# A third seven-product pair in the mixer and attention blocks, with sums of weights made by adding transfers

## The chip, the cores and the metric

The kernel runs on one core of a Trainium2 chip. The metric is the device time of one execution in microseconds (us), the median over several runs. The engines are named as the profile names them: PE (TensorE, with PEld for the loading of its stationary operand), DVE (VectorE), ACT (ScalarE), POOL (GpSimd) and SP (SyncE). SP, ACT and POOL also issue transfers.

## The reference

A decoder trunk of two layers over 256 positions of width 2048, all in float32:

```python
for layer in range(2):
    xn = rms_norm(x, norm_mix[layer])
    x = x + (mixer_mlstm_ssd if layer == 0 else mixer_moba)(xn, ...)
    h = rms_norm(x, norm_ffn[layer])
    x = x + (silu(h @ gate) * (h @ up)) @ down        # 2048 -> 5632 -> 2048
return rms_norm(x, final_norm)
```

Layer 0's mixer projects the normed input with one matrix of 2048 x 12336 (mLSTM queries, keys, values and output gate, two gate rows, and the x, z, B, C and dt columns of a Mamba-2 scan), computes both kinds of heads over chunks, norms and gates them, and multiplies the 4096 resulting columns by one output matrix. Layer 1's mixer is attention with 16 heads and rotary positions; as its blocks are 256 long and there are 256 positions, it is plain causal attention. The work is mostly matrix products of 256 rows with large weight matrices that are read once from memory.

## The kernel before, in words

**Blocks.** Each large product is cut into blocks: the 256 tokens against two strips of 512 columns of a weight matrix (or one strip of each of two matrices), over a depth of 2048 (three feed-forward chunks of 2048, 2048 and 1536 for the down product). `block` (L296) does one. Its depth is cut into pairs of two 128-row tiles; a plan, a string in `PLAN` (L37), has a letter for each pair.

**Precision.** A float32 operand is split into a high part (rounded to the type that TensorE takes, a cast on ACT, L269) and the rest (a subtraction on DVE, L274). A product takes three matmuls of 128 x 128 by 512 columns: high x high, high x low, low x high (`add`, L303 to L307).

**P pairs.** A pair with the letter P has 2 tiles x 2 token halves x 2 strips, that is 8 products, summed in four PSUM banks (`acc_f`).

**S pairs.** A pair with the letter S takes its 2 x 2 x 2 products as one product of 2 x 2 matrices with a seven-product scheme: sums of weights and sums of activations go in, 3 of the products go to `acc_f`, 4 to banks of their own (`acc_e`, L330 to L333). After the last S of a block these four are combined into four tiles `pre` (L335 to L342), and after the block's last pair the `acc_f` banks are added to them (`gathered`, L382). The four `acc_e` banks are those that small products otherwise use in turn (`aux_bank`).

**Weights of a pair** (`weights`, L250). SP loads the pair's weights into two tiles `raw` (six buffers). An S pair needs two first sums of weight tiles, `sums` (two buffers). In the feed-forward parts, where the flag `in_transfers` is set (L942), these come from transfers: SP loads one tile into `sums` (L259), and POOL issues a second transfer that adds another tile onto it (L260); one tile of `raw` is then not loaded (L263). Elsewhere DVE adds them from `raw` (L283). Two more sums (L287, L289) are DVE's in both cases. Then come the casts and subtractions into `wh` and `wl` (six buffers each). These run with a raised priority.

**Sums of activations.** An S pair also needs four sums of the activations' token halves, split into high and low (`activation_sums`, L234), kept in a tile `sk`. They are made once for each pair of a matrix's depth, either when the activations are transposed (L218 to L226) or when an S first asks for them (`summed`, L200). The tiles come from shared homes: `sk` has 3 buffers, `s` 10, `vh` 2, and working tiles (`t2`) 9.

**Order.** Blocks run in this order: two B/C blocks (plan bc), four x/z blocks (xz), qk0, two halves of the first output product (w1), v0, o, qk1, v1, o, two halves of the second output product (w2); feed-forward; av0, aq, aq, av1, aq, aq, two halves of the attention's output product (wo); feed-forward. Smaller work (transposes, convolutions, decays, scores, softmax) is put off with `later` by a number of pairs; after each pair `tick` (L175) runs what is due. From the first S of a block to its last, nothing that was put off runs (`held`), as the banks are taken; it runs after the next pair. Within these orders a scheduler places instructions on each engine by priority, and each engine and queue works through its list in order.

**What lies around the change.** For the mLSTM, `decay_rows` (L653) allocates a tile, issues two transfers on POOL (L657) that spread two rows of cumulated gates over all partitions, and adds a mask on DVE (L661). `mlstm_scores` (L793) calls it and then applies the exponential and the scores. In attention, `rope_block` rotates queries and keys (L979 to L985), `qk_pair` transposes them two pairs later, `attend` makes scores and softmax three and four pairs later (L1010 to L1021), `attend_turn` transposes the probabilities and `attend_out` multiplies by the values, each a pair later; its output is the input `o` of the wo blocks. A norm's square root is taken on POOL (L141).

Of the kernel before, what the change touches and what calls it, by code (L numbers as in the profile page):

```python
# [38 lines left out]
    "v0": "PPPSPSPP", "o": "PPPSPSPP", "qk1": "PPPSPSPP", "v1": "PPPSPSPP", "w2": ("PPPSPSPP", "PPPSPSPP"),  # L39
    "x": "PSPSPSSP", "x0": "PPPSPSSP", "down4": ("PSPSPSSP", "PSPSPSSP"), "down3": ("PSPSPP", "PSPSPP"),  # L40
    "av0": "PPPSPSPP", "aq": "PPPSPSPP", "av1": "PPPSPSPP", "wo": ("PPPPPPPP", "PPPSPSPP"),
# [20 lines left out]
def hybrid_trunk(ctx: ExitStack, tc: tile.TileContext, a: dict, out: bass.AP):  # L62
    nc = tc.nc
# [94 lines left out]
    in_transfers = [False]  # L158
# [91 lines left out]
    def weights(src, row, summed):  # L250
# [6 lines left out]
        if summed and in_transfers[0]:  # L257
            for i, other in enumerate((unit(wa, row + P, ca), unit(wb, row, cb))):
                nc.sync.dma_start(sums[:, i, :], unit(wb, row + P, cb))  # L259
                nc.gpsimd.dma_start(sums[:, i, :], other, accum_op=OP.add)  # L260
        nc.sync.dma_start(raw[0], pair(wa, ca))
        if summed and in_transfers[0]:
            nc.sync.dma_start(raw[1][:, 0, :], unit(wb, row, cb))  # L263
        else:
            nc.sync.dma_start(raw[1], pair(wb, cb))
# [11 lines left out]
        with tc.high_priority(offset=800), tied(last[0], cast[0], *also):  # L277
            if not summed:
                return [low(*parts(r)) for r in raw]
            a, b = raw  # L280
            if not in_transfers[0]:
                for i, other in enumerate((a[:, 1, :], b[:, 0, :])):
                    nc.vector.tensor_add(sums[:, i, :], b[:, 1, :], other)  # L283
            pa = parts(a)
            ps = parts(sums)
            b21, b11 = low(*pa)
            nc.vector.tensor_add(b[:, 1, :], b[:, 0, :], sums[:, 0, :])  # L287
            pb = parts(b)
            nc.vector.tensor_add(a[:, 0, :], a[:, 0, :], b[:, 1, :])  # L289
            t1, t3 = low(*ps)  # L290
            pt = parts(a, 1)
            b22, t2_ = low(*pb)
            t4, = low(*pt)
            return b21, b11, b22, t3, t1, t2_, t4
# [481 lines left out]
    vh, em = {}, {}  # L776
# [4 lines left out]
    def v_block(g, plan, wait):  # L781
        for i in range(2):
            later(wait + i, ("e", g), mlstm_scores, g, i)
# [9 lines left out]
    def mlstm_scores(g, i):  # L793
        need(("qk", g))
        es = decay_rows(4 * g + 2 * i, s_home)
        em[2 * g + i] = es
# [101 lines left out]
    def ffn(xt, r, wg_, wu_, wd, name, finish, begin=None):  # L898
# [43 lines left out]
        in_transfers[0] = True  # L942
# [9 lines left out]
        in_transfers[0] = False  # L952

    xt2, ss2, finish_ffn0 = next_x("2", G_MIX1, {1: sk_home, 3: sk_home, 5: sk_home})
# [205 lines left out]
```

## Time and profile before

| | |
|---|---|
| runs | 2546.05, 2547.03, 2551.55 us; median 2547.03 |
| the profiled execution | 2547.64 us, of which the trace's span is 2545.9 |
| PE busy | 2534.9 us (100%) |
| DVE busy | 2236.4 us (88%) |
| ACT busy | 1571.5 us (62%) |
| POOL busy | 283.7 us (11%) |
| moved | 593.72 MB, 233 GB/s on average |

The span is that of the core's instructions; some 1.7 us of the time lie around it. A row by stretches gives start and end, its length, busy time of PE, PEld, DVE, ACT and POOL with the number of instructions behind each, the granted clock of PE, the share of time in which the 16 DMA engines were busy, and GB/s. A row of a group gives line, engine, operation, output and inputs, shape, count, then busy us and mean ns, then the idle time before it with what ended it. A row of waits gives who waited for whom: us in total, times, longest. A row of the timeline starts with its start and its length in us. Matmuls are pipelined: one shows about 390 ns, while the next starts before it ends, so that their pace is read from their starts or their count.

### The profile page before, as it was taken

Reading aid. Unit: us, or ns where it says so; the run is one execution under the profiler, and the core shown is the slowest. Engines: PE = TensorE matmul, PEld = TensorE weight load, DVE = VectorE, ACT = ScalarE, POOL = GpSimd, SP = SyncE. Lnnn points to the kernel's source line nnn. Section 1 sums busy time; section 2 is a strip of 40 time slices with the busy share of each in tenths; the row PEclk is TensorE's granted clock in tenths of the full one; section 3 lists DMA queues with packets and bytes.
Section 4 is the critical chain, followed back from the end, with each engine's and each line's share of the span. In section 5 each row is a group of like instructions: output and inputs, shape, how many; then the busy total and the mean of one; then the engine's idle time right before and its main releaser. Section 6 shows DMA issues by size and latency. Waiting matters only on the chain.

```text
span 2545.9 us, 34058 instructions
## 1 busy us (share of the span) xinstructions
PE 2534.9 (100%) x11595; PEld 2090.3 (82%) x11595; DVE 2236.4 (88%) x2995; ACT 1571.5 (62%) x2108; POOL 283.7 (11%) x356
## 2 busy tenths in 40 slices
PE   9999999999999999999999999999999999999998
PEld 8888888888888888888888888888888888888887
DVE  6877789887799999999999989878899999999998
ACT  6566766565666665666566655656566656665664
POOL 2101200000001111111111000000011111111110
PEclk9999999999999999999999999999999999999999
DMA  8656656566578999999999756555689999999995
GB/s 282 184 166 190 197 165 218 178 189 212 158 219 238 276 271 285 277 282 264 287 271 280 249 174 196 176 163 176 203 224 283 262 288 279 275 272 289 290 270 169
DMA packets 312158, 593.72 MB, mean 233 GB/s; under 512 B 24184, under 2 KB 26752, under 8 KB 311984
## 3 DMA queue, kind: packets, MB, share of 16 engines
q1 hardware_dynamic: 271248, 515.12, 61.3%
q0 software_dynamic: 39552, 74.58, 16.6%
q8 instruction: 91, 1.49, 0.2%
q10 hardware_dynamic: 1184, 1.84, 0.2%
q14 instruction: 83, 0.68, 0.1%
HBM read 589.32 MB, written 2.14 MB: 232 GB/s over the span
## 4 chain that ended last, share of the span: by engine, by line
PE 94%; issue 3%; DVE 2%; DMA 1%; ACT 0%; POOL 0%; POOLq 0%; DVEq 0%; ACTq 0%
PE acc_f L305 24%; PE acc_f L307 24%; PE acc_f L306 24%; PE acc_e L305 6%; PE acc_e L307 5%; PE acc_e L306 5%; PE p_tr L215 1%; PE p_y L727 1%; DVE wl L274 1%; PE p_qt L772 0%; PE p_num L815 0%; DMA raw<-in_l_ffn_down 0%; PE p_cv L468 0%; PE p_o L1036 0%; PE p_qk L1008 0%
## 5 line engine op out<-in xcount | busy, mean ns | idle before, releaser
L269 ACT CAST wh<-raw 128x1024 fp32r<-128x1024 f32 (+1 forms) x1070 | 1041.7, 989 | 676.6 <-PE acc_f L307 298.2
L274 DVE TENSOR_TENSOR wl<-raw,wh 128x1024 fp32r<-128x1024 f32 (+1 forms) x1070 | 1206.5, 1142 | 203.7 <-ACT wh L269 193.0
L305 PE MATMUL acc_f<-wh,x 128*128 128x512 f32 x1204 | 472.2, 392 | 0.0
L306 PE MATMUL acc_f<-wl,x 128*128 128x512 f32 x1204 | 471.2, 391 | 0.0
L307 PE MATMUL acc_f<-wh,x 128*128 128x512 f32 x1204 | 471.0, 391 | 0.0
L305 PE MATMUL acc_f<-wh,xa 128*128 128x512 f32 x708 | 281.2, 397 | 0.0
L307 PE MATMUL acc_f<-wh,xa 128*128 128x512 f32 x708 | 276.5, 391 | 0.0
L306 PE MATMUL acc_f<-wl,xa 128*128 128x512 f32 x708 | 276.4, 390 | 0.0
L307 PEld LDWEIGHTS acc_f<-wh,x 128*128 128x128 f32 x1204 | 226.2, 188 | 46.4
L306 PEld LDWEIGHTS acc_f<-wl,x 128*128 128x128 f32 x1204 | 226.2, 188 | 46.3
L305 PEld LDWEIGHTS acc_f<-wh,x 128*128 128x128 f32 x1204 | 226.3, 188 | 45.8
L269 ACT CAST wh<-sums 128x1024 fp32r<-128x1024 f32 x160 | 168.6, 1054 | 143.3 <-PE acc_f L307 71.3
L274 DVE TENSOR_TENSOR wl<-sums,wh 128x1024 fp32r<-128x1024 f32 x160 | 195.3, 1221 | 18.4 <-ACT wh L269 18.4
L260 POOL DMA_DIRECT2D sums<-in_l_ffn_gate x86 | 74.6, 868 | 1135.0 <-DVE wl L274 491.4
L305 PE MATMUL acc_e<-wh,sk 128*128 128x512 f32 x480 | 190.2, 396 | 0.0
L306 PE MATMUL acc_e<-wl,sk 128*128 128x512 f32 x480 | 187.4, 390 | 0.0
L307 PE MATMUL acc_e<-wh,sk 128*128 128x512 f32 x480 | 186.5, 391 | 0.0
L307 PEld LDWEIGHTS acc_f<-wh,xa 128*128 128x128 f32 x708 | 132.9, 188 | 28.1
L306 PEld LDWEIGHTS acc_f<-wl,xa 128*128 128x128 f32 x708 | 133.2, 188 | 26.9 <-DVE wl L274 0.4
L305 PEld LDWEIGHTS acc_f<-wh,xa 128*128 128x128 f32 x708 | 133.1, 188 | 26.0
L287 DVE TENSOR_TENSOR raw<-raw,sums 128x512 f32<-128x512 f32 x160 | 109.6, 685 | 7.9 <-DMA sums<-in_l_ffn_down 4.9
L305 PEld LDWEIGHTS acc_e<-wh,sk 128*128 128x128 f32 x480 | 90.1, 188 | 28.4 <-ACT xg L221 6.8
(337 smaller groups left out, 3981.6 us busy)
## 6 DMA issues: line engine op xcount, KB each, us to landing
raw<-in_l_w_in SPq DMA_DIRECT2D x192, 512.0 KB, 4.4
raw<-in_l_ffn_gate SPq DMA_DIRECT2D x176, 512.0 KB, 6.3
raw<-in_l_ffn_down SPq DMA_DIRECT2D x136, 512.0 KB, 6.8
raw<-in_l_w_qkv SPq DMA_DIRECT2D x96, 512.0 KB, 4.6
raw<-in_l_ffn_up SPq DMA_DIRECT2D x90, 512.0 KB, 6.3
sums<-in_l_ffn_up SPq DMA_DIRECT2D x172, 256.0 KB, 4.6
raw<-in_l_w_out SPq DMA_DIRECT2D x64, 512.0 KB, 4.8
sums<-in_l_ffn_gate POOLq DMA_DIRECT2D x86, 256.0 KB, 6.6
```

The source lines that it names most:

```text
L215: turned = nc.tensor.transpose(pt[:, i * T + t * P:i * T + (t + 1) * P], src[t][:, i * P:(i + 1) * P], ident)
L260: nc.gpsimd.dma_start(sums[:, i, :], other, accum_op=OP.add)
L269: cast[0] = nc.scalar.copy(h[:, :n, :], of[:, :n, :]).ins
L274: last[0] = nc.vector.tensor_sub(l[:, :n, :], of[:, :n, :], h[:, :n, :].bitcast(F32)).ins
L287: nc.vector.tensor_add(b[:, 1, :], b[:, 0, :], sums[:, 0, :])
L305: nc.tensor.matmul(dst, ah, bh, start=start, stop=False, **kw)
L306: nc.tensor.matmul(dst, ah, bl, start=False, stop=False, **kw)
L307: nth[0] = nc.tensor.matmul(dst, al, bh, start=False, stop=stop, **kw).ins
L727: nc.tensor.matmul(py[:, o0:o0 + SHD], e[:, lo:lo + P], y[:, st, hs], start=st == 0, stop=st == t, skip_group_check=True)
```

## The change: what it does

Three things, in one edit. First, the flag `in_transfers` goes: every S pair, in mixer and attention too, gets its two first sums of weights by adding transfers, and the DVE additions of L283 go. Second, the plans: fourteen blocks change from two S (pairs 3 and 5) to three (pairs 3, 5 and 6): v0, both o, qk1, v1, both w2, av0, the four aq, av1 and the second wo. The first wo block changes from no S to two, in pairs 1 and 2. As the attention input's pairs 3, 5 and 6 are now the S pairs there, `next_x("2", ...)` makes sums of activations for these and no longer for pair 1. Third, `v_block` calls `decay_rows` for both head pairs ahead of its block, and `mlstm_scores` takes the tile from there.

```diff
 PLAN = {
     "bc": "PPPPPPPP", "xz": "PPPPPPPP", "qk0": "PPPPPPPP", "w1": ("PSPSPSPP", "PSPSPSPP"),
-    "v0": "PPPSPSPP", "o": "PPPSPSPP", "qk1": "PPPSPSPP", "v1": "PPPSPSPP", "w2": ("PPPSPSPP", "PPPSPSPP"),
+    "v0": "PPPSPSSP", "o": "PPPSPSSP", "qk1": "PPPSPSSP", "v1": "PPPSPSSP", "w2": ("PPPSPSSP", "PPPSPSSP"),
     "x": "PSPSPSSP", "x0": "PPPSPSSP", "down4": ("PSPSPSSP", "PSPSPSSP"), "down3": ("PSPSPP", "PSPSPP"),
-    "av0": "PPPSPSPP", "aq": "PPPSPSPP", "av1": "PPPSPSPP", "wo": ("PPPPPPPP", "PPPSPSPP"),
+    "av0": "PPPSPSSP", "aq": "PPPSPSSP", "av1": "PPPSPSSP", "wo": ("PSSPPPPP", "PPPSPSSP"),
 }
...
         if summed:
             sums = home("sum")([P, 2, STRIP], "sums")
-        if summed and in_transfers[0]:
             for i, other in enumerate((unit(wa, row + P, ca), unit(wb, row, cb))):
                 nc.sync.dma_start(sums[:, i, :], unit(wb, row + P, cb))
                 nc.gpsimd.dma_start(sums[:, i, :], other, accum_op=OP.add)
         nc.sync.dma_start(raw[0], pair(wa, ca))
-        if summed and in_transfers[0]:
+        if summed:
             nc.sync.dma_start(raw[1][:, 0, :], unit(wb, row, cb))
...
             a, b = raw
-            if not in_transfers[0]:
-                for i, other in enumerate((a[:, 1, :], b[:, 0, :])):
-                    nc.vector.tensor_add(sums[:, i, :], b[:, 1, :], other)
             pa = parts(a)
...
     def v_block(g, plan, wait):
         for i in range(2):
+            em[2 * g + i] = decay_rows(4 * g + 2 * i, s_home)
             later(wait + i, ("e", g), mlstm_scores, g, i)
...
     def mlstm_scores(g, i):
         need(("qk", g))
-        es = decay_rows(4 * g + 2 * i, s_home)
-        em[2 * g + i] = es
+        es = em[2 * g + i]
...
-    xt2, ss2, finish_ffn0 = next_x("2", G_MIX1, {1: sk_home, 3: sk_home, 5: sk_home})
+    xt2, ss2, finish_ffn0 = next_x("2", G_MIX1, {3: sk_home, 5: sk_home, 6: sk_home})
```

More of the change, by code (lines that the diff above doesn't have):

```diff
@@ L157, in hybrid_trunk @@
     also, evacuated = [], []
-    in_transfers = [False]
     last, cast, nth, fresh = [None], [None], [None], [None, None]
@@ L940, in down @@
                         finish(s)
-        in_transfers[0] = True
         first = 0
@@ L951, in ffn @@
             first += n
-        in_transfers[0] = False
-    xt2, ss2, finish_ffn0 = next_x("2", G_MIX1, {1: sk_home, 3: sk_home, 5: sk_home})
+    xt2, ss2, finish_ffn0 = next_x("2", G_MIX1, {3: sk_home, 5: sk_home, 6: sk_home})
     ffn(xt1, r1, a["l0_ffn_gate"], a["l0_ffn_up"], a["l0_ffn_down"], "a", finish_ffn0)
```

## The prediction

> **What bounds the kernel now.** I read the page first, then the waits of TensorE, then busy times by stretch.
>
> ```profile
> span 2545.9 us, 34058 instructions
> PE 2534.9 (100%) x11595; PEld 2090.3 (82%) x11595; DVE 2236.4 (88%) x2995; ACT 1571.5 (62%) x2108; POOL 283.7 (11%) x356
> PEclk9999999999999999999999999999999999999999
> PE 94%; issue 3%; DVE 2%; DMA 1%; ACT 0%; POOL 0%; POOLq 0%; DVEq 0%; ACTq 0%
> ```
> TensorE is busy throughout, at full clock, and carries 94% of the chain that ended last. A pipelined matmul counts as busy while it only drains, so I look for its waits and its pace:
>
> ```profile
> PE warm L122 <- POOL phase L105: 1.0, 1, 1.0
> PE acc_f L305 <- ACT wh L269: 0.8, 1, 0.8
> PE p_cols L645 <- ACT colsrc L635: 0.4, 1, 0.4
> PE acc_e L305 <- DVE x L149: 0.3, 1, 0.3
> ```
> ```profile
> 1510.00:1548.00 38.00, 38.00 (x169) 31.49 (x168) 28.90 (x33) 19.31 (x21) 0.00 (x0) 1.00 0.59 188
> 724.60:768.60 44.00, 44.00 (x204) 36.59 (x203) 39.02 (x56) 27.35 (x40) 3.54 (x4) 1.00 0.74 231
> 768.60:812.00 43.40, 43.40 (x201) 36.01 (x200) 39.23 (x57) 30.61 (x44) 6.96 (x7) 1.00 0.78 218
> ```
> In the whole span TensorE waits 2.5 us (starts of blocks, here and below, are found by counting the matmuls along the plans). The first stretch lies in an attention block that has only 512-column matmuls: 38.0 / 168 = 0.2262 us per matmul, one behind the other. The second stretch, from block start to block start, is the last mixer block (plan PPPSPSPP); the third is the first feed-forward block (PPPSPSSP). Both carry 16 transposes besides. The third S takes three matmuls out (204 to 201) and 0.60 us, where 3 x 0.2262 = 0.68. So this kernel's time is its count of matmuls, and an added S pair is worth 0.68 us wherever its inputs arrive in time.
>
> **What the change takes off TensorE.** A P pair issues 8 products x 3 passes = 24 matmuls, an S pair 21. By the plans, v0, o (twice), qk1, v1, w2 (two blocks), av0, aq (four), av1 and the second output block gain one S each: 14. The first output block gains two. 16 x 3 = 48 matmuls, 48 x 0.2262 = **10.9 us**. The Trainium skill ("TensorE: Matmul & The Clock Gate", section "Back-to-back issue gap") gives about 131 ns for a sustained 512-column matmul; by that page the 48 would be worth an estimated 6.3 us. The trace's 226 ns disagrees with it here, and I go by the trace.
>
> **What it moves off and onto the other engines.**
>
> ```profile
> L274 DVE TENSOR_TENSOR wl<-raw,wh 128x1024 fp32r<-128x1024 f32 x910 | 1104.9, 1222 | 182.5 <-ACT wh L269 173.8
> L274 DVE TENSOR_TENSOR wl<-raw,wh 128x512 fp32r<-128x512 f32 x160 | 110.1, 688 | 21.2 <-ACT wh L269 19.3
> L287 DVE TENSOR_TENSOR raw<-raw,sums 128x512 f32<-128x512 f32 x160 | 109.6, 685 | 7.9 <-DMA sums<-in_l_ffn_down 4.9 <-DMA sums<-in_l_ffn_gate 2.9
> L388 DVE TENSOR_TENSOR pre<-acc_f,pre 128x512 f32<-128x512 f32 x152 | 98.7, 684 | 3.2 <-PE acc_f L307 3.1
> L283 DVE TENSOR_TENSOR sums<-raw 128x512 f32<-128x512 f32 x68 | 43.8, 685 | 0.0
> L237 DVE TENSOR_TENSOR sf<-xg 128x128 f32<-128x128 f32 x40 | 11.4, 285 | 0.2
> L985 DVE TENSOR_TENSOR rot<-rot,swp 128x512 f32<-128x512 f32 x16 | 11.0, 686 | 0.1
> 2200.00:2400.00 200.00, 200.00 (x886) 163.87 (x885) 186.99 (x223) 120.69 (x134) 33.38 (x38) 1.00 0.97 283
> ```
> VectorE: the 68 additions of L283 go (-43.8 us). An S pair costs it 3 x 1.222 + 0.688 + 2 x 0.685 = 5.72 us, a P pair 2 x 1.222 = 2.44: 16 x 3.28 = +52.5. Five sums of activations are new (input pair 6, mixer-output pair 6, attention-output pairs 1, 2, 6), each 0.685 + 4 x 0.285 + 0.685 = 2.5: +12.5. The first output block's eight extra 512-wide combinations at 0.684 add 5.5. Together +27 us over some 780 us of mixer and attention. The feed-forward stretch quoted last has VectorE at 93% (186.99 of 200) with TensorE at its full pace; mixer and attention stay below that on average. So VectorE costs nothing, except in bursts (below). ScalarE gains 16 x 1.6 us of casts at 62% load: nothing. The attention input trades pair 1's sums for pair 6's: the same count, made at av0's start, some 30 us before they are used: nothing.
>
> ```profile
> q1 hardware_dynamic: 271248, 515.12, 61.3%
> q0 software_dynamic: 39552, 74.58, 16.6%
> 500.00:600.00 100.00, 100.00 (x461) 83.37 (x460) 77.59 (x103) 65.87 (x105) 5.16 (x8) 1.00 0.57 180
> sums<-in_l_ffn_up POOLq DMA_DIRECT2D x86, 256.0 KB, 8.1
> L260 POOL DMA_DIRECT2D sums<-in_l_ffn_up x86 | 99.2, 1153 | 16.3 <-DMA sums<-in_l_ffn_up 16.1 <-issue 0.2
> SPq L259 <- DVE wl L274: 502.1, 122, 7.1
> ```
> DMA: plain transfers take 0.613 x 2545.9 / 515.12 = 3.03 us of all 16 engines per MB, adding ones (queue q0) 0.166 x 2545.9 / 74.58 = 5.67. A P pair loads 1.05 MB (3.2 us); an S pair with sums in transfers 1.31 MB plain and 0.52 MB adding (6.9 us). Check: a feed-forward block of 4 P and 4 S makes 40.4 us in about 42 (180 x 0.2262 and some transposes), which is 0.96, where the row of 2200 to 2400 says 0.97. A mixer block of 5 P and 3 S makes 36.6 us in 43: 0.85, up from the 0.57 of the row, and below what feed-forward bears. Cost nothing; cover lost only if an adding byte cost almost twice as much.
>
> GpSimd and SyncE: 50 S pairs bring 100 adding issues to GpSimd's queue, which was nearly empty there, and 100 more to SyncE's. SyncE's loads stand behind issues that wait for a free sums buffer; in feed-forward they do so for 502.1 us and TensorE doesn't feel it: 0. At 1.15 us each GpSimd has room, but it is in order, and a sum has to be asked for two transfers (8.1 us the adding one) ahead: an issue waiting for its plain half, or for a free sums buffer, holds up what stands behind. Behind it stand the four square roots of the mLSTM norm, the memsets of the column of ones, and the decay rows. The rows are issued a block's start earlier instead of with the scores:
>
> ```profile
> 552.31 2.92 POOL L657 DMA_DIRECT2D rows<-scr  x4 [0.40 <-issue]
> ```
> These are the second group's four issues, and they already lie 35 us ahead of the block that uses them (it starts at 586), as their buffers are free then. So the move is worth nothing now; it only keeps them from the back of the new queue. Their mask additions (L661) move along. Cost 0.
>
> **Bursts in attention.** From the first S to the last of a block no deferred task runs. The hold grows by one pair in 14 blocks, and the first output block gets a hold over pairs 1 and 2. Two places suffer: av1 and the first output block, which begin with the rotary work, softmax and transposes of the block before.
>
> ```profile
> 1615.87 0.68 DVE L985 TENSOR_TENSOR rot<-rot,swp 128x512 f32<-128x512 f32 x1
> 1616.55 0.27 PE L772 MATMUL p_qt<-ident,rot 128*128 128x128 f32 x1
> 1764.66 0.39 PE L1007 MATMUL p_qk<-aq,aq 128*128 128x128 f32 x2
> 1772.41 0.38 PE L1007 MATMUL p_qk<-aq,aq 128*128 128x128 f32 x2
> 1778.97 0.59 PE L1036 MATMUL p_o<-pT,av 128*128 128x256 f32 x2
> 1781.38 0.44 PE L1027 MATMUL p_pt<-ident,prob 128*128 128x128 f32 x2
> ```
> (a) av1: the transposes of the rotated tokens (1616.55) start as VectorE ends the rotary work (1615.87 + 0.68), 4 us ahead of the first S: no slack. Half of the softmax now falls into that stretch, and the additions of L283 leave it. From 0 to 2 us; I take 0.5.
> (b) First output block (1744 to 1799): scores of heads 0 and 1 at 1764.66 give outputs at 1778.97, 14.3 us later; heads 2 and 3 follow with a last transpose at 1781.38. With the hold all four heads start together behind pair 3, about 1770: outputs near 1784 and, with two more softmaxes in line (5 to 6 us of ScalarE), 1790. Pairs 6 and 7, which need them, would start about 1786.5 and 1792. Slack of one or two us each, less a cast and a subtraction: 0 to 4 us; I take 1.
> (c) The same block's pair 1, about 6.5 us in, needs activation sums, 2.5 us of VectorE, when that still has four L388 (2.7), twelve rotary operations (0.686 each: 8.2) and two S pairs' weights (11.4) to do. Three of seven products need no sums and can go first. In the second output block such sums are already late:
>
> ```profile
> 1814.54 0.68 DVE L205 TENSOR_TENSOR xg<-o 128x512 f32<-128x512 f32 x1
> 1817.01 0.68 DVE L146 TENSOR_TENSOR sk<-sf,sk 128x512 fp32r<-128x512 f32 x1
> ```
> Its first S begins about 1817.1, yet nothing is seen to wait for long. From 0 to 8 us; nearer the quoted rows, so 1.5. None of the three can be a gain, since TensorE waits only 2.5 us in all now.
>
> **Sum.** The profiled execution took 2547.6 us (span 2545.9). 2547.6 - 10.9 + 0.5 + 1.0 + 1.5 = 2539.7. It lies 0.6 us above the median of the runs, 2547.0, so the median should be **2539.1**.
>
> **Rivals.**
> *Attention gives the gain back.* If (a) to (c) come at their upper halves, 8 to 12 us instead of 3, the time is 2544 to 2548. For it: the bunching above. Against: instructions of later pairs are seen between transposes, so a late input needn't stop TensorE. At 6 us or so: 2542.
> *GpSimd's order stops the mixer* (slower).
>
> ```profile
> POOL sums L260 <- DMA sums<-in_l_ffn_up: 315.8, 44, 13.9
> L141 POOL TENSOR_TENSOR rrm<-rs,mhalf 128x4 f32<-128x4 f32 x4 | 4.1, 1019 | 181.6 <-DVE rs L140 181.6
> 514.80 1.01 POOL L141 TENSOR_TENSOR rrm<-rs,mhalf 128x4 f32<-128x4 f32 x1 [6.93 <-DVE rs L140]
> ACT wh L269 <- PE acc_f L307: 369.4, 263, 3.1
> ```
> In feed-forward an adding issue sat 7.2 us on average, at most 13.9, until its plain half had landed. The four roots of L141 lie next to an S (514.80; the S begins at 516.6); VectorE and ScalarE wait for them in order, and the weights queue behind. ScalarE's casts wait for TensorE to free buffers (369.4 us), so weights are ahead: six tiles, a pair or more ahead, 5.5 us. A wait of 13.9 then costs 8.4, four times 34: 2547.0 - 10.9 + 34 = 2570. Above 8.2 us of wait each it is slower than before. The average of 7.2 would cost 7 us and leave 2543. Against: a root issued before the adding DMA never meets it. The Trainium skill has GpSimd's queue as a strict FIFO of 8 ("TensorE: Matmul & The Clock Gate", opening table); the trace's waits agree with order, its depth isn't shown.
> *The change has no effect*, since something else sets the pace: 2547. The two block rows speak against it.
> *DMA becomes the bound* in mixer and attention: with adding bytes at twice 5.67 a block needs 45.5 us instead of 43, 14 times +2.5: 2571.
>
> **Numbers.** Forecast 0.74; attention gives it back 0.13; GpSimd's order 0.06; no effect 0.05; DMA 0.02. About 0.2% (5 us) is what a measurement of this kernel can tell from no change. Faster: 0.74 (the forecast; a mild case of the first rival lies near the edge, 2542). Same: 0.13 + 0.05 = 0.18. Slower: 0.06 + 0.02 = 0.08. The range runs from all 10.9 us with nothing lost, 2536.1, less 0.6 for run-to-run, to the first rival's middle, 2546.
>
> **What would show it.** Right: 48 fewer matmuls in the group counts, L283 gone, 176 groups of sums in place of 160, mixer blocks 0.6 to 0.7 us shorter, DMA share about 0.8 there, TensorE without waits but in the first output block. Wrong: gaps of TensorE in the o blocks, behind casts that stand behind L141; waits of `acc_e` for `sk` or of `p_qk` in the first output block beyond 4 us; DMA share near 1 with waits for `sums` in mixer blocks.

## The result, and the profile after

The changed kernel takes 2562.1 us (median of 4 runs, 2561.3 to 2566.2), the kernel before 2547.5 beside it: a ratio of 1.0058, 95% interval 1.0041 to 1.0075. It is 14.6 us slower; 2539.1 was forecast, and the range ended at 2546.

From the page of the kernel after:

```profile
span 2559.5 us, 34553 instructions
PE 2532.6 (99%) x11547; PEld 2081.9 (81%) x11547; DVE 2256.6 (88%) x3029; ACT 1592.9 (62%) x2146; POOL 369.9 (14%) x456
PE 90%; DVE 5%; DMA 3%; issue 1%; ACT 1%; POOL 0%; DVEq 0%; POOLq 0%; ACTq 0%; SPq 0%
q0 software_dynamic: 53952, 100.80, 22.5%
```

TensorE runs exactly 48 matmuls fewer, yet the span is 13.6 us longer, and its share of the chain fell from 94% to 90%. The waits of TensorE say who took the rest:

```profile
PE p_cw L569 <- DMA cw_rows<-in_l_ssd_conv_w: 3.2, 1, 3.2
PE acc_e L300 <- DVE x L149: 2.6, 2, 1.3
PE p_pt L1020 <- ACT prob L1014: 2.4, 2, 1.6
PE acc_f L300 <- DVE pre L383: 1.7, 3, 0.7
PE p_tr L214 <- DVE pre L847: 1.4, 2, 1.1
PE acc_e L300 <- ACT pT L1022: 1.4, 1, 1.4
```

Before, the longest of them was 1.0 us. (Of the two waits of `acc_e` for `x`, one is in av0; the other is in the last down block of the first feed-forward part, where a block also loses 1.3 us in run 12, without any added S or transfer.) Now the blocks, cut at their first matmul by counting along the plans. First v0 and an o block, then the first output block and the first half of w2; the kernel before:

```profile
450.20:495.10 44.90, 44.90 (x204) 37.33 (x203) 40.30 (x56) 22.80 (x25) 0.00 (x0) 1.00 0.60 190
495.10:542.40 47.30, 47.30 (x211) 39.44 (x210) 33.85 (x47) 32.56 (x57) 2.03 (x2) 1.00 0.55 174
1744.10:1798.90 54.80, 54.80 (x269) 45.05 (x268) 36.53 (x64) 33.38 (x74) 0.00 (x0) 1.00 0.49 153
680.50:724.50 44.00, 44.00 (x203) 36.40 (x202) 41.61 (x61) 26.28 (x35) 0.00 (x0) 1.00 0.59 190
```

and the kernel after:

```profile
455.20:499.40 44.20, 44.20 (x200) 36.76 (x199) 40.51 (x60) 24.32 (x27) 5.24 (x6) 1.00 0.74 208
499.40:546.10 46.70, 46.70 (x209) 38.93 (x208) 34.34 (x47) 32.62 (x58) 7.93 (x8) 1.00 0.74 220
1748.40:1812.70 64.30, 58.77 (x271) 46.10 (x270) 52.45 (x96) 40.03 (x80) 3.50 (x4) 0.95 0.62 181
683.70:730.70 47.00, 45.03 (x201) 35.29 (x199) 42.77 (x65) 28.10 (x37) 5.23 (x6) 1.00 0.85 242
```

v0 and o give the 0.7 us that an added S is worth, with TensorE never idle. The first output block has two added S and is 9.5 us longer; VectorE's work there rose from 36.5 to 52.5 us. "Loss" means below how much longer a block has become, once the 0.68 us that each added S should save are counted. The losses come to 13.6 + 10.9 = 24.5 us:

| block | before | after | loss |
|---|---|---|---|
| second B/C block | 54.90 | 59.88 | 5.0 |
| first output block of attention | 54.81 | 64.24 | 10.8 |
| last rotary block (part of its small matmuls now lies in the block after it) | 49.21 | 46.74 | -1.8 |
| first w2 block | 44.04 | 47.00 | 3.6 |
| second output block | 44.51 | 45.76 | 1.9 |
| qk1 | 43.96 | 44.88 | 1.6 |
| av0 | 44.60 | 44.91 | 1.0 |
| the two blocks x0 behind w2 and wo | 86.82 | 88.33 | 1.5 |
| all others together (single ones from -1.3 to 1.3) | | | 0.9 |

**The second B/C block has no S in its plan.** GpSimd's queue shows what holds it, the kernel before first:

```profile
40.65 0.73 POOL L141 TENSOR_TENSOR r<-rs,mhalf 128x2 f32<-128x2 f32 x1 [9.78 <-DVE rs L140]
41.35 0.62 POOL L572 DMA_DIRECT2D cw_rows<-in_l_ssd_conv_w  x1
```
```profile
40.58 0.73 POOL L141 TENSOR_TENSOR r<-rs,mhalf 128x2 f32<-128x2 f32 x1 [9.83 <-DVE rs L140]
45.87 1.86 POOL L258 DMA_DIRECT2D sums<-in_l_w_out  x2 [4.56 <-DMA sums<-in_l_w_out]
48.03 0.85 POOL L258 DMA_DIRECT2D sums<-in_l_w_out  x1 [0.30 <-issue]
53.65 0.86 POOL L258 DMA_DIRECT2D sums<-in_l_w_out  x1 [4.76 <-DMA sums<-in_l_w_out]
54.19 0.89 POOL L567 DMA_DIRECT2D cw_rows<-in_l_ssd_conv_w  x1
```

The first sums of w1, a block that starts at 370 us, are asked for from 40 us on, because both `sums` buffers are free and nothing ties the fetch to its use. The adding transfers wait for their plain halves, and behind them the convolution's weights `cw_rows` leave at 54.2 and not at 41.4. They also land later, 6.8 us after their issue where it was 3.0: with 3.0 they would have been there at 57.2, just before TensorE came to wait for them (57.9). TensorE stands still for 3.2 us and is then granted half its clock for 3.4; the wait and half of that stretch make 4.9 of the 5.0 us. The rows by stretch of the kernel after, here and in the first output block:

```profile
61.10:64.50 3.40, 3.40 (x9) 2.72 (x10) 0.29 (x1) 0.00 (x0) 0.00 (x0) 0.51 1.05 408
1761.00:1767.80 6.80, 4.44 (x10) 2.58 (x10) 6.80 (x14) 2.97 (x6) 1.75 (x2) 0.50 0.71 170
```

In the second stretch VectorE is busy throughout, TensorE for two thirds of it and at half speed.

**The first output block.** VectorE around its start, before and after (equal lengths of time):

```profile
1735.00:1770.00 35.00, 35.00 (x176) 28.67 (x175) 28.04 (x51) 20.01 (x40) 0.00 (x0) 1.00 0.55 181
```
```profile
1740.00:1775.00 35.00, 29.47 (x124) 22.05 (x123) 34.14 (x60) 18.97 (x33) 5.23 (x6) 0.90 0.84 234
```

and what it does in the kernel after from 1747.81 on:

```profile
1747.81 0.68 DVE L282 TENSOR_TENSOR raw<-raw,sums 128x512 f32<-128x512 f32 x1
1748.40 1.22 DVE L272 TENSOR_TENSOR wl<-sums,wh 128x1024 fp32r<-128x1024 f32 x1
...
1752.73 1.23 DVE L272 TENSOR_TENSOR wl<-raw,wh 128x1024 fp32r<-128x1024 f32 x1 [0.17 <-ACT wh L267]
1753.87 0.55 DVE L1003 TENSOR_TENSOR prob<-p_qk,phase 128x384 f32<-128x384 f32 x1
...
1767.82 0.68 DVE L204 TENSOR_TENSOR xg<-o 128x512 f32<-128x512 f32 x1
```

VectorE is busy for 34.14 of 35 us. The weights of the two S pairs, at their raised priority, go first; the sums of the attention output come only at 1767.82. The softmax at 1753.87 is that of the last two heads of the third group of four. In the kernel before, it ran ahead of the block:

```profile
1739.00 1.01 DVE L1010 TENSOR_TENSOR prob<-p_qk,phase 128x384 f32<-128x384 f32 x2
```

There the scores of these heads were made at 1735.5, behind pair 6 of the rotary block before. Now pair 6 is an S, the hold lasts one pair longer, and the scores come behind pair 7, at 1747.3. So TensorE, in order, meets the transposes of these probabilities (`p_pt`) in the first S pair and waits. It then waits 1.4 us more for a bank: `acc_e` uses those of the small products, and one of them holds a transposed tile until ScalarE has copied it to `pT`. ScalarE in turn had waited for VectorE's rotary work, from which `pT` reads nothing:

```profile
1763.71 1.08 ACT L1022 COPY pT<-p_pt 128x384 f32<-128x384 f32 x2 [1.65 <-DVE rot L978]
```

What it waited for there is probably one of the nine working tiles that both use; no run changes their number. TensorE's waits in this block add up to 5.5 us, all of them in its first S pair. From pair 3 on, where the last group of four heads has its scores and outputs, it waits for nothing.

### The profile page after: what moved, and what is told of

It reads as the page before. It is cut to its first block, busy times and chain, and to the rows that moved or that the text cites. A ratio compares the mean times of both kernels' runs of the same rounds, so it can differ in the third digit from the quotient of the medians.

```text
span 2559.5 us, 34553 instructions
## 1 busy us (share of the span) xinstructions
PE 2532.6 (99%) x11547; PEld 2081.9 (81%) x11547; DVE 2256.6 (88%) x3029; ACT 1592.9 (62%) x2146; POOL 369.9 (14%) x456
## 3 DMA queue, kind: packets, MB, share of 16 engines
q0 software_dynamic: 53952, 100.80, 22.5%
## 4 chain that ended last, share of the span: by engine, by line
PE 90%; DVE 5%; DMA 3%; issue 1%; ACT 1%; POOL 0%; DVEq 0%; POOLq 0%; ACTq 0%; SPq 0%
PE acc_f L300 22%; PE acc_f L302 22%; PE acc_f L301 22%; PE acc_e L300 6%; PE acc_e L302 6%; PE acc_e L301 6%; DVE wl L272 2%; PE p_tr L214 2%; DMA raw<-in_l_ffn_down 1%; PE p_y L722 1%; ACT wh L267 1%; PE p_qt L767 0%; PE p_num L810 0%; DMA raw<-in_l_ffn_gate 0%; DVE xin L914 0%
## 5 line engine op out<-in xcount | busy, mean ns | idle before, releaser
L300 PE MATMUL acc_f<-wh,x 128*128 128x512 f32 x1168 | 457.1, 391 | 0.7 <-DVE pre L383 0.7
L301 PE MATMUL acc_f<-wl,x 128*128 128x512 f32 x1168 | 456.8, 391 | 0.0
L302 PE MATMUL acc_f<-wh,x 128*128 128x512 f32 x1168 | 456.6, 391 | 0.0
L300 PE MATMUL acc_f<-wh,xa 128*128 128x512 f32 x678 | 270.4, 399 | 0.0
L267 ACT CAST wh<-sums 128x1024 fp32r<-128x1024 f32 x176 | 185.1, 1052 | 134.9 <-PE acc_f L302 84.8
L302 PE MATMUL acc_f<-wh,xa 128*128 128x512 f32 x678 | 265.4, 391 | 0.0
L301 PE MATMUL acc_f<-wl,xa 128*128 128x512 f32 x678 | 265.2, 391 | 0.0
L300 PEld LDWEIGHTS acc_f<-wh,x 128*128 128x128 f32 x1168 | 219.3, 188 | 46.0 <-DVE pre L383 1.2
L302 PEld LDWEIGHTS acc_f<-wh,x 128*128 128x128 f32 x1168 | 219.4, 188 | 45.0
L272 DVE TENSOR_TENSOR wl<-sums,wh 128x1024 fp32r<-128x1024 f32 x176 | 214.5, 1219 | 20.4 <-ACT wh L267 19.9
L300 PE MATMUL acc_e<-wh,sk 128*128 128x512 f32 x528 | 209.0, 396 | 2.7 <-DVE x L149 2.6
L301 PE MATMUL acc_e<-wl,sk 128*128 128x512 f32 x528 | 206.1, 390 | 0.0
L302 PE MATMUL acc_e<-wh,sk 128*128 128x512 f32 x528 | 203.1, 391 | 0.0
L282 DVE TENSOR_TENSOR raw<-raw,sums 128x512 f32<-128x512 f32 x176 | 120.3, 683 | 5.8 <-DMA sums<-in_l_ffn_down 3.4
```

The costliest lines, as they stand in the source:

```text
L267: cast[0] = nc.scalar.copy(h[:, :n, :], of[:, :n, :]).ins
L272: last[0] = nc.vector.tensor_sub(l[:, :n, :], of[:, :n, :], h[:, :n, :].bitcast(F32)).ins
L300: nc.tensor.matmul(dst, ah, bh, start=start, stop=False, **kw)
L301: nc.tensor.matmul(dst, ah, bl, start=False, stop=False, **kw)
L302: nth[0] = nc.tensor.matmul(dst, al, bh, start=False, stop=stop, **kw).ins
```

## The experiments

The texts on record call the theories by letters. A: separate stalls, each with a place and a price, the conv rows behind the first sums (5 us) and the first output block (9 to 11 us) the largest; against it, a general price of the adding transfers or of the pairs. C: VectorE's bursts at the ends of blocks. The others are explained where they stand. Each kernel ran beside the kernel before (2546.3, 2546.5, 2547.1, 2546.8 and 2546.4 us in the five groups). Where no ratio is given, the result is a single run.

**1. The first output block as before.**

```diff
-"wo": ("PSSPPPPP", "PPPSPSSP")
+"wo": ("PPPPPPPP", "PPPSPSSP")
```

> The changed kernel with the first output block back at no S (PPPPPPPP); all else of the change stays. Theory A (separate local stalls): the block took 64.2 us changed and 54.8 before, so this gives back 9.4 us: 2562.1 - 9.4 = 2552.7. Theory B (the adding transfers and their queues slow mixer and attention in general, and the first output block only shows it most): the block gets its 54.8 us back only in part, say 3 to 6 us: 2556 to 2559, and other blocks stay late. The wait of TensorE for the probabilities (p_pt) and the half-clock stretch at 1761 to 1768 us should go under A.

2553.5 us (2552.3 to 2557.7), ratio 1.0029 (1.0017 to 1.0040). The block is back at 56.4 us, without a wait of TensorE and at full clock; the two S pairs there cost 8.6 us of the 14.6 (7.4 if each kernel is set against the kernel before beside it). A holds.

**2. The conv rows issued by ScalarE.**

```diff
-        nc.gpsimd.dma_start(cw_rows, a["l0_ssd_conv_w"]...
+        nc.scalar.dma_start(cw_rows, a["l0_ssd_conv_w"]...
```

> The changed kernel with one transfer, that of the convolution rows, issued by ScalarE instead of GpSimd, so that it no longer stands behind four adding issues. Theory A: the second B/C block goes from 59.9 us back to 54.9 and nothing else moves: 2562.1 - 5.0 = 2557.1, full clock there. Theory B (the rows are late because the weights of the first output product are loaded into a busy memory at that time): the rows land as late as now on another queue; 2561 to 2562.

2561.6 us, 1.0061 (1.0046 to 1.0076): no gain. ScalarE reached the issue only at 54.3 us, so the rows came hardly earlier (and took 6.0 us to land, from a queue without adding transfers); the block's loss fell from 5.0 to 2.6 us, and other blocks took it back. As a proof of A it failed; the same idea is tried better in run 9.

**3. All the plans, but the sums made by VectorE as before** (the kernel before, with the `PLAN` after and the sums of activations for pairs 3, 5 and 6).

> The plans of the change alone: all sixteen added S pairs, but mixer and attention make the first two sums on VectorE, as before, and decay rows are fetched where they were. Theory A: no adding issue stands ahead of the convolution rows (5.0 us back), the first output block stalls as in the change or a little more, since VectorE has more to do (two more additions, 1.4 us, for each S): 2556 to 2560. Theory B: without the transfers the sixteen pairs pay: 2536 to 2545.

2585.4 us, 1.0152 (1.0137 to 1.0167): far over both expectations. The second B/C block is as before, but the last mixer blocks and the first output block lose 8.5, 11.7 and 16.9 us, and the second output block 6.9. TensorE's longest wait in the last mixer blocks:

```profile
PE acc_f L305 <- DVE pre L388: 11.1, 1, 11.1
```

So the transfers do what they are for: without them the added pairs cost 39 us, with them, their own price included, 15. The two more additions for each S are VectorE's, and it is VectorE that TensorE waits for.

**4. The transfers and the decay rows, with the plans of before** (the kernel after with the old `PLAN`).

> The change with the plans of before: 34 S pairs of mixer and attention get their sums by adding transfers, decay rows are fetched ahead, no S is added. Theory A: only the wait for the convolution rows is added: 2547.5 + 5.0 = 2552.5, mixer blocks unchanged to 0.3 us each. Theory B: the transfers cost several us beyond that, 2556 or more, with late weights in many blocks. Below 2547 neither holds.

2556.8 us, 1.0041 (1.0026 to 1.0056), 4 us over A's figure. The second B/C block loses 7.3 us here and qk1 3.3, without one added S in the kernel; all other blocks next to nothing.

**5. Sums held back, first try.** Two placeholders take the `sums` buffers and are read behind the third x/z block.

```diff
+    kept = [home("sum")([P, 2, STRIP], "sums") for _ in range(2)]
+    for k in kept:
+        nc.gpsimd.memset(k[:, 0, :1], 0.0)
...
+        if s == 2:
+            let_go = tiny([P, 2], "let_go")
+            for i, k in enumerate(kept):
+                nc.vector.tensor_copy(let_go[:, i:i + 1], k[:, 0, :1])
```

> The changed kernel, with both sums buffers kept occupied by placeholders from the start until the third x/z block (two one-column memsets on GpSimd, two one-column copies on VectorE), so that the sums of the first output product can't be fetched in the B/C blocks. Theory A (the convolution rows stand behind adding issues on GpSimd's queue, and beside their bytes): the second B/C block takes 54.9 us again instead of 59.9, no half clock at 61 us, and all else stays: 2562.1 - 5.0 = 2557.1. Rival (the rows are late for another reason, such as a working buffer that comes free late): the block stays at 58 us or more, 2560 to 2562.

2566.9 us, 1.0078 (1.0063 to 1.0093). It tells nothing: the reads had no late input, the scheduler put them early, the sums were fetched as early as in the kernel after, and `cw_rows` left at 56.9.

**6. Twelve added S in place of sixteen.**

```diff
-    ... "w2": ("PPPSPSSP", "PPPSPSSP"),   "wo": ("PSSPPPPP", "PPPSPSSP")
+    ... "w2": ("PPPSPSPP", "PPPSPSSP"),   "wo": ("PPPPPPPP", "PPPSPSPP")
```

> The changed kernel with no S in the first output block, and two S instead of three in the first block of the mixer's output product and in the second block of the attention's: 12 added S pairs are left. Theory C (VectorE's work bunches in blocks that also split new activations and make new sums, and there the third S doesn't fit): against the kernel without S in the first output block, 2553.5, the first of these blocks gives back 4.7 + 0 us, down to 44.0, the other 1.2 to 1.9; 2547 to 2548. Rival D (the late weights come from the adding transfers, which stay): each block keeps half of its loss or more, 2550 to 2553.

2549.4 us (2546.5 to 2551.6), 1.0010 (1.0000 to 1.0019). Losses of the first w2 block 1.3 us (5.4 in run 1, which has the same block with three S), of the second output block none (1.9). The time lies between the two expectations, 1.4 us above C's and 0.6 below D's; by the blocks C holds, as much less than half of each loss is left. The second B/C block still loses 5.9.

**7. The softmax at a raised priority, the full change** (`with tc.high_priority(offset=1600)` around L1000 to L1014).

> The whole change, with the operations of a softmax (mask, maxima, exponential, scaling) at a raised priority, ahead of the weights of S pairs. Theory E (in the first output block TensorE waits for the probabilities because VectorE serves the weights of two S pairs first): the stall ahead of the transposes of the probabilities, 5.5 us with the wait behind it, goes, and with it part of the half-clock stretch; the block takes 57 to 60 us instead of 64.2. Rival (it is the sums of activations that come late): 62 to 64.

2576.2 us (a single run). The first output block takes 66.2 us, and av1 and the rotary block behind it lose some 7 more. Neither expectation is met. The wait on `p_pt` goes, as E has it; in its place TensorE waits for a bank, as ScalarE's copies out of it come late:

```profile
PE acc_e L300 <- ACT pT L1023: 5.7, 1, 5.7
```
```profile
1776.60 1.02 ACT L1023 COPY pT<-p_pt 128x384 f32<-128x384 f32 x2 [4.77 <-DVE rot L978]
```

The probabilities were transposed by 1769.4, but the copies had to wait for the rotary work, which VectorE now does behind them and the weights. Late weights are only 1.5 us of the block's waits. So this order doesn't help; that none would, the run doesn't show.

**8. The first output block without its own sums of activations** (`oT.sums` set to two sums of the attention input, so that this part of the result is another one).

> The whole change, but the two S pairs of the first output block use sums of activations that are there already, those of the attention's input: two sums of activations are left out, and the output is not the reference's. Theory E: the stall ahead of the transposes of the probabilities stays and the block takes 60 to 63 us. Rival (late sums): the block falls to 56 us or less.

2561.2 us (a single run); the block 61.95, within E's expectation. Those sums are worth 64.24 - 61.95 = 2.3 us by this one trace (in the change and runs 2, 5 and 9 the same block takes 64.2 to 66.3); the wait on `p_pt` stays.

**9. Sums held back, second try.** The placeholders are now read together with the convolution's weights, which come from `cw_rows`.

```diff
     nc.vector.tensor_scalar(convw, pcw[:, :P], 0.5, None, op0=OP.mult)
+    let_go = tiny([P, 4], "let_go")
+    for i, k in enumerate(kept):
+        nc.vector.tensor_add(let_go[:, 2 * i:2 * i + 2], k[:, 0, :2], convw[:, :2])
```

> The full change, with two short-lived placeholders in the sums buffers that VectorE reads for the last time right behind the halving of the convolution's weights, so that the first sums of w1 can be fetched only after cw_rows has been (the placeholders are four tiny VectorE instructions; nothing is left out). Theory A (GpSimd, in order, holds cw_rows behind accumulating transfers that wait for their plain halves): cw_rows is issued at 40 to 42 us as in the kernel before, the wait of p_cw goes, the half-speed clock at 61 us with it, the second B/C block is back from 59.9 to 54.9 to 55.2 us, and the time is 4.7 to 5.5 below the change's 2562.1: 2556.6 to 2557.4. Rival D (the block is late because more bytes move in that stretch): the sums still come, only later, and the block stays over 57.

2558.0 us (2555.9 to 2560.2), 1.0040 (1.0025 to 1.0055): 4.1 us of the 14.6 are gone (3.7 against the kernels before beside them). GpSimd's queue of this kernel:

```profile
40.37 0.73 POOL L144 TENSOR_TENSOR r<-rs,mhalf 128x2 f32<-128x2 f32 x1 [9.79 <-DVE rs L143]
41.06 0.62 POOL L570 DMA_DIRECT2D cw_rows<-in_l_ssd_conv_w  x1
```

The block takes 54.85 us, the wait and the half clock at 61 us are gone. A's cause of the first loss is shown, with one addition: the edit moves the adding transfers behind `cw_rows` (65.8 to 73.9 us, still in this block), and so takes away both the order that held the rows and the traffic beside which they landed late (2.9 us now). (The time falls a little less than the block, as this profile's first w2 block loses 8.3 us where the change's lost 3.6, and the first output block 12.8 instead of 10.8; in the kernels with transfers and three S the first w2 block varied from 2.7 to 8.3.)

**10. Twelve added S, and the conv rows first** (runs 6 and 9 together).

> Twelve added S pairs (those of w2's first block, of the first output block and of the second output block back as in the kernel before), with all sums of weights by transfers, decay rows ahead, and the placeholders that keep cw_rows first. By theories A and C together: 2549.4 of the kernel with these plans less 5.9 of its second B/C block: 2543 to 2544, faster than the kernel before by 2.5 to 3.5 us. If the two losses are not separate (the stall in the second B/C block only moves), 2547 to 2549.

2545.1 us (11 runs, 2542.0 to 2548.3), 0.9991 (0.9982 to 1.0000) of the kernel before: 2 us faster, at the edge of what can be told, and 1 us over what was expected. The largest waits of TensorE in its trace:

```profile
PE acc_e L303 <- DVE x L152: 1.3, 1, 1.3
PE warm L125 <- POOL phase L105: 1.0, 1, 1.0
PE p_tr L217 <- DVE pre L853: 0.8, 1, 0.8
```

**11. The same, with the gate's two instructions at a raised priority** (tanh and L853, `offset=1600`).

> As the kernel with twelve added pairs and the placeholders, and besides, the gate's tanh and the instruction that multiplies by it (the two ahead of the transposes p_tr<-ident,pre) at a raised priority of 1600, above the 800 of the weights. Theory C (the low halves and sums of weights stand ahead of the gate on VectorE at the ends of qk1 and of the first w2 block): the waits of 1.7 and 1.1 us on p_tr<-ident,pre go, and the time is 1.5 to 2.8 below the kernel without it, 2540.5 to 2542.5. Rival E (whoever goes first, the other is late, as for the softmax): the waits move to the low halves and the time is within 1 us of the kernel without it, or above.

2545.6 us, 0.9994 (0.9985 to 1.0003). No gain. In qk1 the wait of 0.8 us on `p_tr` goes, but TensorE waits 1.4 us for a bank that VectorE has yet to read and 1.1 for low halves of weights; the block loses 3.7 us in place of 1.5, and the first w2 block 2.9 in place of 0.6. The rival holds (its letter E stands for another theory here than in run 7): as there, putting one thing first makes another late.

**12. The decay rows ahead, alone, on the kernel before.**

> The kernel before with one part of the change alone: the decay rows are fetched ahead, at the start of their block and not when the scores are computed. The prediction priced it at nothing: within 0.5 us of the kernel before. Rival: eight fetches per pair of heads that now stand earlier in GpSimd's queue hold what follows: up to 2 us slower.

2547.6 us, 1.0001 (0.9992 to 1.0010): nothing, as predicted.

**13. The first output block's two S without low halves of their weights.**

```diff
-    def weights(src, row, summed):
+    def weights(src, row, summed, bare=False):
...
         def low(of, h, n):
+            if bare:
+                return [(h[:, i, :], h[:, i, :]) for i in range(n)]
...
-                b21, b11, b22, t3, t1, t2_, t4 = weights(src, row + 2 * j * P, True)
+                b21, b11, b22, t3, t1, t2_, t4 = weights(src, row + 2 * j * P, True, plan.startswith("PSS"))
```

The rounded weight takes the place of its low half, so that this part of the result is another one.

> The full change, but the two seven-product pairs of the first output block leave out the low halves of their weights (the rounded weight is used in the place of its low half, so that TensorE multiplies as often and the transfers are the same, and VectorE does not subtract: 5 instructions less per pair). Theory F (the amount of VectorE's work around the softmax): the wait on p_pt and the half-speed clock go, and the first output block takes 54 to 57 us where the change's took 64.2; the time is near 2553 to 2555. Rival G (the order of held pairs and softmax, or the sums of the attention output, whatever VectorE has to do): the block stays over 61.

A single run, 2564.7 us. The block takes 60.4 us and lies between both expectations: its loss falls from 10.8 to 6.9, the wait on `p_pt` goes, the half clock lasts 3.4 and not 6.8 us. What is left of TensorE's waits there:

```profile
PE acc_f L303 <- DVE wl L274: 1.1, 1, 1.1
PE acc_e L302 <- ACT pT L1024: 0.9, 1, 0.9
```

The edit leaves out four subtractions per pair, some 8.7 us of VectorE's work (3 x 1.222 + 0.688 each pair). So these are 3.9 us of the loss, the shorter half clock included, but not all. The whole time shows nothing of it, as in this run the second B/C block lost 2.2 and the first w2 block 4.6 us more than in the change.

**14. The two S pairs two places later** (`"PPPSSPPP"`).

> The full change with the two seven-product pairs of the first output block two places later, PPPSSPPP in the place of PSSPPPPP: the same work, but the softmax of the last two heads and their turns now stand behind the held pairs. Theory F: the burst on VectorE still meets the softmax, the block takes 58 to 65 us. Rival G (the place decides): either 54 to 56, when the weights are now served after the first softmax, or well over 65, when the turns of the last heads are held back too long.

A single run, 2556.6 us. The block takes 63.8 us, its loss 10.4 as against 10.8. The place in the block does not decide; F's expectation holds and G's doesn't. Two things differ all the same: the clock stays at full speed throughout the block, so that the half clock isn't needed for a loss of this size, and the second output block, which lost 1.9 us, now loses nothing.

**15. The transfers without added S, and the conv rows first** (runs 4 and 9 together).

> All transfers of sums and the decay rows ahead, none of the added seven-product pairs, and the placeholders that keep cw_rows ahead of the first sums. If the transfers cost nothing of themselves (the prediction's row 'DMA and GpSimd nothing'), what is left of the 9.4 us that the transfers alone cost is the loss in qk1: 2546 to 2550. If they have a price of their own, 2553 or more.

2550.8 us, 1.0017 (1.0008 to 1.0026). Between the two expectations: the transfers with the decay rows' move have a price of some 4 us, though that move alone has none (run 12). qk1 loses 3.3 and v1 1.6. GpSimd's queue in this kernel ahead of that, and then the waits of VectorE, of SyncE's queue and of TensorE there:

```profile
554.25 1.75 POOL L261 DMA_DIRECT2D sums<-in_l_w_in  x2 [4.89 <-DMA sums<-in_l_w_in]
555.32 3.59 POOL L658 DMA_DIRECT2D rows<-scr  x4
```
```profile
DVE rows L662 <- DMA rows<-scr: 5.8, 1, 5.8
```
```profile
SPq L262 <- DVE rows L662: 9.5, 1, 9.5
```
```profile
PEld acc_f L303 <- ACT wh L270: 2.4, 1, 2.4
```

The decay rows of v1 again stand behind two adding transfers (they left at 552.31 before, and landed in 5.1 us; here at 555.32, in 7.7). VectorE reaches the addition of their mask and stands still for 5.8 us, where it didn't wait before. SyncE's load behind that waits 9.5 us for its buffer, and TensorE 2.4 us for weights at 589. In the full change the same wait of VectorE is 3.7 us.

**16. As 10, with qk1 and av0 back at two S.**

> Ten added seven-product pairs: the kernel with twelve and placeholders, with qk1 and the first value block of attention back at two as well, the two blocks that showed no gain. By its blocks (qk1 +0.83, av0 +0.24): about 1.1 us below its 2545.1: 2543 to 2545, 0.9980 to 0.9993 of the kernel before.

2547.0 us, 1.0006 (0.9997 to 1.0015). The expectation fails: qk1 with two S loses 3.7 us and the first w2 block 2.5 where run 10 lost 1.5 and 0.6. The block's loss doesn't come from its own third S.

**17. As 15, with the mask of v_block's decay rows added by GpSimd.**

```diff
-            nc.vector.tensor_add(rb[:, :, lo:lo + P], rb[:, :, lo:lo + P],
+            nc.gpsimd.tensor_add(rb[:, :, lo:lo + P], rb[:, :, lo:lo + P],
```

> All transfers of sums, none of the added pairs, the placeholders that keep cw_rows first, and the four additions of the mask to the decay rows of the value blocks done by GpSimd and not by VectorE, so that whoever waits for the fetched rows is not VectorE. Theory H (VectorE, in order, waits 5.8 us for the decay rows that GpSimd's queue held behind the accumulating transfers, and the weights of the next block are late behind it): the wait of 2.4 us on the rounded weights at the end of qk1 goes with its half-speed clock, qk1 and v1 together lose under 1.5 us where they lost 4.9, and the time is 3 to 4 us below 2550.8: 2547 to 2548. Rival I (the weights are late because the transfers take the DMA engines): qk1 and v1 keep their 4.9 us and the time stays at 2550 to 2551.

2560.9 us, 1.0059 (1.0043 to 1.0074), 10 us more and not 3 to 4 less. The edit put the wait elsewhere: VectorE no longer waits for the rows, but ScalarE, which applies the exponential, does, and the weights' casts stand behind it; qk1 loses 3.8. And GpSimd, waiting for the rows of the first group at 377 us, makes ScalarE wait there too, in a block that had no loss. The waits around qk1, and then around the block w1 at 382:

```profile
ACT rows L667 <- POOL rows L662: 5.5, 1, 5.5
```
```profile
ACT rows L667 <- POOL rows L662: 7.6, 2, 7.4
PE acc_e L303 <- ACT qk L774: 7.0, 1, 7.0
```

**18. The same edit on kernel 10.**

> The kernel with twelve added pairs and the placeholders (2545.1), with the mask of the decay rows added by GpSimd. Theory H: qk1's loss of 0.83 us turns into the gain of 0.68 or near it, the time is 1 to 2 us lower: 2543 to 2544, 0.9982 to 0.9990 of the kernel before. Rival: VectorE's work behind the decay rows fills the gap and the wait on p_tr<-ident,pre stays; 2545.

2554.5 us, 1.0033 (1.0020 to 1.0045), 9 us over kernel 10, with 11 us lost in w1. So in both runs theory H is not tested as meant: late rows stop whichever engine meets them first. That rows behind the adding transfers are what makes qk1 lose is read from the traces of 15 and 17, where an in-order engine waits 5.5 to 5.8 us for them, and not shown: a version that fetches them in time was not run, and rival I (the DMA engines' time) is not excluded for the part of the wait that is the longer landing.

## Why the prediction was wrong, by its own steps

The sum put all losses at 3.0 us; the blocks show 24.5. Two steps failed: the cost of 0 for GpSimd's queue, and the terms for the bursts, which looked at the wrong pairs and left out the ends of blocks.

- **48 matmuls at 0.2262 us: right.** The count fell by 48, and v0, o and others show 0.68 us per S. What was wrong is what 24.5 us of losses did to a gain of 10.9.
- **GpSimd and SyncE, "cost 0": the step that failed first.** The list of what stands behind the adding transfers named roots, memsets and decay rows and left out `cw_rows`, 320 us ahead of the first S. The prediction had the sums asked for two transfers ahead of their use; with two free buffers they were asked for as soon as the queue came to them. The price is 5.0 us in that block; run 9 takes 4.1 us back. The rival *GpSimd's order* had the mechanism, but put it at the roots of L141: the o blocks that hold them lose 0.13 us at most.
- **The decay rows, "cost 0": right alone, wrong together.** Run 12 gives nothing for the move itself. But it does not keep them ahead of the adding transfers: they left 3 us later than before in run 15, and an engine waited for them.
- **Bursts (b) and (c), 1.0 + 1.5 us: the step that failed with the largest price.** The block's loss is 10.8 us (1.6 of it is moved from the block before, as run 1's block shows; run 1 gives 8.6 for the two S). (b) took the last four heads and their outputs, and priced them by ScalarE's softmax and the slack of the outputs at pairs 6 and 7; there TensorE waits for nothing. It knew that the hold grows, but not what this does in the rotary block before: two heads of the third group move over the border, and their softmax then stands on VectorE behind the weights of the S pairs. Of the 9.2 us that are not moved, 5.5 are the waits in the first S pair, and an estimated 2.2 the half clock (half of the 4.44 us in which TensorE was busy at half speed); 1.5 are not taken apart. By cause, (c), the sums, is 2.3 by run 8, near the 1.5 (it let three products go ahead of the sums; in the kernel's order two do, and the second of them needs a bank of `acc_e`), and VectorE's subtractions are 3.9 by run 13. Each of these two is from one trace, and they need not add up. Neither the order of run 7 nor the place of run 14 helps. How much the working tiles are worth, and what two S there would cost behind a rotary block with two S, stays open.
- **"VectorE costs nothing, except in bursts": right on average, wrong on where the bursts are.** VectorE is 20 us busier, where 27 was worked out: the lengths of instructions were added up, but the rows above show the next one starting before the last has ended (1747.81 + 0.68, the next at 1748.40). An estimate by their starts gives 21. The term had no place for the ends of blocks: the first w2 block, the second output block and the blocks x0 behind them lose 7 us too, at the ends of blocks where an S pair's weights meet the gate and the combination of the banks; by run 6 most of it goes when the first w2 block and the second output block keep two S.
- **(a) av1, 0.5 us: right**, no loss above 0.1 (the rotary blocks before and behind it differ by -1.3 and +1.3 us, which cancel).
- **DMA: right, as far as TensorE's waits show.** The adding bytes took 0.225 x 2559.5 / 100.80 = 5.71 us per MB (5.67 before), and the first w2 block's share is 0.85, as worked out, at no wait for `sums` on TensorE.
- **No step priced the clock.** The wait of 3.2 us in the second B/C block is followed by 3.4 us at half clock, and the waits of the first output block by 6.8.
- **The rivals were taken one at a time.** *Attention gives the gain back* at 8 to 12 us and *GpSimd's order* came true together, and the sum of both left the range. That each came near a price on record (10.8 for 8 to 12, 5.0 for the 7 at an average wait) is partly luck: the first stall was not at the pairs that were priced, and the second not at the roots. A further 8.7 us, in qk1, av0, the ends of blocks and the rest, was in neither.

## What to carry to other kernels

A transfer that waits in an in-order queue costs what stands behind it, however far its own use lies: list everything in that queue from the moment its buffers are free, not from a block before its use. An engine that is 88% busy on average can be at 98% in one stretch, and there a pair that spares TensorE 0.68 us and asks 3.3 more of VectorE didn't pay, in any order that was tried: put such a trade only where the stretch has room, and look at each block by itself. Where a hold grows, ask also what it pushes into the next block. A stall has a second price when the clock falls behind it.

## What the runs showed of the hardware

The granted clock after a stall comes in steps. After TensorE's waits of 7.0 us (run 17) and 8.5 us (run 18) in w1:

```profile
378.60:385.40 6.80, 2.95 (x7) 2.37 (x8) 3.93 (x6) 6.60 (x14) 1.75 (x3) 0.50 0.23 78
```
```profile
377.40:387.60 10.20, 4.53 (x11) 3.56 (x12) 5.51 (x8) 8.48 (x16) 2.80 (x4) 0.50 0.22 78
```

The stretches at half clock in these runs last 3.4 us (the change, runs 13 and 15), 6.8 (the change, run 17), 10.2 (run 18) or 13.7 (run 9's first output block), one to four times the same length. The lengths agree with the Trainium skill ("TensorE: Matmul & The Clock Gate", Part 1: The HAM clock gate), which has the clock halved and released by windows of 3413 ns that run on their own. What sets a stretch off does not come out of these runs: a wait of 2.4 us (run 15) was followed by one, and so were waits of 0.6 to 1.6 us within some 7 us (the change's first output block), while in run 14's, with single waits of up to 1.5 us, there was none.
